# Pinning a pair's preparation to program order and moving the weights' low parts ahead on VectorE, in a two-layer RWKV-7 and attention encoder

## The chip, the cores and the metric

The kernel runs on one core of one Trainium2 chip. The metric is the device time in microseconds of one execution; lower is better. TensorE is PE in the profile (its weight loads PEld), VectorE is DVE, ScalarE is ACT, GpSimd is POOL and SyncE, which issues the DMAs, is SP.

## The reference

Two layers over 256 tokens of width 2048, all in float32. Each layer normalizes, multiplies by one input matrix, runs two groups of heads side by side and multiplies by one output matrix:

```python
for l in range(DEPTH):
    h = rms_norm(x, norm_g[l])
    proj = jnp.einsum('btd,dc->btc', h, w_in[l])
    rw_in, g_rw, q, k_at, v_at, g_at = jnp.split(proj, col_splits, axis=-1)
    rw_in = bidir_token_shift(rw_in, shift_mu[l])
    r, k, v, xw, xa = jnp.split(rw_in, rw_splits, axis=-1)
    y_rw = rwkv7_branch(r, k, v, xw, xa, ...)      # 16 heads of 64, a scan in each direction
    ...
    y_at = window_attention(qh, kh, vh, sink[l])   # 16 heads, 4 of keys and values
    mix = jnp.concatenate([y_rw * silu(g_rw), y_at * silu(g_at)], axis=-1)
    x = x + jnp.einsum('btc,cd->btd', mix, w_out[l])
return rms_norm(x, final_g)
```

One step of the scan, per head, with a 64x64 state S:

```python
s_kk = einsum('bhvk,bhk->bhv', S, kk_t)
S = S * w_t - s_kk * (a_t * kk_t) + v_t * k_t
y_t = einsum('bhvk,bhk->bhv', S, r_t)
```

The decay w, the rate a and the normalized key kk are made from the projections by two low-rank products, tanh, exp and a sum over each head.

## The kernel before, in words

**The gemm stream.** Both matrix products are one stream of steps (`Stream`, `gemm`). A tile is 128 output columns by 256 tokens, made in 16 steps over K = 2048. Each step is three matmuls (L273, L274, L275), because every operand is split into a high and a low part: high weights by high x, high weights by low x, low weights by high x. The third one needs `lo`. Weights come in halves of 8 steps. For each half, `wload` issues a DMA into `raw` (3 buffers), and `wsplit` makes `hi` on ACT (L215) and `lo` on DVE (L216), in two pieces of 512 columns, into 2 buffers each. A half is loaded and split (traced, that is) when 2 steps of the half before are left (`PREFETCH`). When a tile is done its eviction is traced: for k, v and r one DVE multiply (L400), an ACT scale (L401) and two DVE shifts (L402, L403); v also splits the low-rank weights of its pair (L442 on ACT, L443 on DVE); for the gate L411 to L413. The accumulators have 2 banks in PSUM.

**The windows.** The RWKV heads are done in 8 pairs. `window` cuts 64 gemm steps, four tiles, into 14 slots. In each slot it first advances the generators that are due, in this order: `scan_b` (the scan along 4 chunks, one step a slot), `scan_i` (what is inside a chunk; inverts triangular blocks by doubling, one level in two slots: L815, L817, L821, L823, then L824 and L825 on DVE), and last `scan_p`. Then it runs that slot's gemm steps. A pair passes `scan_p` in one window, `scan_i` in the next, `scan_b` behind it, so in the steady state three pairs are in work at once.

**The preparation, `scan_p`.** Its steps are in slots 4, 5, 6, 7, 8, 9, 10, 11 and 13 (`STAGE_P`):

- slot 4: the low-rank matmuls (L623 to L625), then on ACT L645, L648 twice, L650, L652
- slot 5: on DVE L655 and two running sums (L658)
- slot 6: head sums on PE (L629), ACT exponentials L664, L665, DVE reciprocal L667 and L668
- slot 7: DVE L675, L676, ACT L677 to L679
- slots 8, 9 and 10: DVE L681, L684; L686, L687 and ACT L688; L690 and ACT L694, L695
- slots 11 and 13: DVE L699, L700; head sums on PE and L705

Its results BK and MV are first read by `scan_i` at L720, in slot 0 of the next window.

**What sets the order.** The order of PE is the order in which the program is traced (`manual_schedule`). The order of each other engine is made ahead of time by a list scheduler: of the instructions that its own timing model holds ready, it issues the one with the lowest priority number, and that number is the instruction's place in the traced program. `tc.high_priority(offset=n)` moves a block's numbers n places ahead. `scan_b` has 95 (`PRIO_B`), the norm 100, all else none. So a piece whose inputs are ready early may be issued long before the place where it is traced. Once made, an engine's order is fixed in the program. The `lo` of L216 is traced in `wsplit` behind its `hi`:

```python
A.activation(hi[:, q], raw[:, q], AF.Copy)
V.tensor_tensor(lo[:, q], raw[:, q], hi[:, q].bitcast(F32), op=ALU.subtract)
```

At the end of a layer's windows come attention (`scores`, `flip`, `values`) and the output product, which is gemm stream alone.

Of the kernel before, what the change touches and what calls it, by code (L numbers as in the profile page):

```python
# [9 lines left out]
F32 = mybir.dt.float32  # L10
# [5 lines left out]
AF = mybir.ActivationFunctionType  # L16
ALU = mybir.AluOpType
# [4 lines left out]
T = 256  # L22
# [9 lines left out]
DECAY_C = -0.5 * float(np.exp(-0.5))  # L32
# [3 lines left out]
P_NG, P_MU0, P_MU1, P_KK, P_KA, P_RK, P_LG, P_LB, P_A0 = 0, 16, 42, 68, 76, 84, 92, 100, 108  # L36
P_N = 124
NSH = 26
# [12 lines left out]
    [0, 2, 5, 7, 8, 10, 12, 13],  # L51
]
PRIO_B = 95
PREFETCH = 2


# [72 lines left out]
def hybrid_trunk_kernel(ctx, tc, xT, wi, wv, wo, par, fing, dup, iup, sink, pos, cst, out):  # L129
    nc = tc.nc  # L130
    V, A, G, PE, SY = nc.vector, nc.scalar, nc.gpsimd, nc.tensor, nc.sync
# [73 lines left out]
    def wload(src):  # L205
        raw = wrp.tile([128, 1024], F32, tag="raw", name="raw")
        SY.dma_start(out=raw, in_=src)
        return raw

    def wsplit(raw):  # L210
        hi = wsp.tile([128, 1024], F32R, tag="hi", name="hi")
        lo = wsp.tile([128, 1024], F32R, tag="lo", name="lo")
        for i in range(2):
            q = slice(i * 512, (i + 1) * 512)
            A.activation(hi[:, q], raw[:, q], AF.Copy)  # L215
            V.tensor_tensor(lo[:, q], raw[:, q], hi[:, q].bitcast(F32), op=ALU.subtract)  # L216
        return hi, lo

    def halves(src, first=None):
        return [lambda: wsplit(first if first is not None else wload(src[0])), lambda: wsplit(wload(src[1]))]  # L220

    class Stream:


        def __init__(self):
            self.q = []
            self.ready = []
            self.timers = []
# [159 lines left out]
    def queue_inputs(l):  # L388
# [218 lines left out]
    def layer(l):  # L607
        L = layers[l]
        prm = lambda o, j: PR[:, l, o + j : o + j + 1]
        dpm = lambda o, j: DP[:, l, o + j : o + j + 1]  # L610
# [11 lines left out]
        def low_rank(o, w, x):  # L622
            PE.matmul(o, w[0], x[0], start=True, stop=False)  # L623
            PE.matmul(o, w[0], x[1], start=False, stop=False)
            PE.matmul(o, w[1], x[0], start=False, stop=True)  # L625

        def head_sums(o, x):
            for r in half:
                PE.matmul(o[r, 0:T], bones[r, r], x[r, 0:T], start=True, stop=True)  # L629


        def scan_p(p, t):
            K, VV, R, iu, du = t["k"], t["v"], t["r"], t["iu"], t["du"]
            dd = lambda x: x.rearrange("p (d x) -> p d x", d=2)
            two = lambda x: x.unsqueeze(1).to_broadcast([128, 2, T])
            c8 = lambda x: x.rearrange("p (n j) -> p n j", j=64)

            pza = wpair("pza")
            pz, pa = pza[:, 0], pza[:, 1]
            for d in range(2):  # L640
                low_rank(pz[:, d * T : (d + 1) * T], [a[0 : RANK + 1, d, :] for a in du], [a[0 : RANK + 1] for a in L.TW])
            LW = st("lw", [2 * T])
            for d in range(2):
                low_rank(pa[:, d * T : (d + 1) * T], [a[0:RANK, d, :] for a in iu], [a[0:RANK] for a in L.XA])
            A.activation(LW, pz, AF.Tanh, scale=0.5)  # L645
            TH = st("th", [2 * T])
            for d in range(2):
                A.activation(TH[:, d * T : (d + 1) * T], pa[:, d * T : (d + 1) * T], AF.Tanh, scale=0.5, bias=dpm(NSH + 16, d * 8 + p))  # L648
            sq = st("t1", [T], bufs=3)
            A.activation(sq, K, AF.Square, scale=prm(P_KK, p))  # L650
            KR = st("kkr", [T])
            A.activation(KR, K, AF.Identity, scale=prm(P_KK, p))  # L652
            yield

            V.tensor_scalar(LW, LW, 1.0, None, op0=ALU.add)  # L655
            msk = MSK.rearrange("p c j -> p (c j)")
            for x in (LW[:, 0:T], LW[:, T : 2 * T][:, ::-1]):
                V.tensor_tensor_scan(x, msk, x, 0.0, op0=ALU.mult, op1=ALU.add)  # L658
# [5 lines left out]
            A.activation(PP.rearrange("p d c j -> p (d c j)"), LW, AF.Exp, scale=DECAY_C)  # L664
            A.activation(IP.rearrange("p d c j -> p (d c j)"), LW, AF.Exp, scale=-DECAY_C)  # L665
            KD = st("kd", [T])
            V.reciprocal(KD, pk[:, 0:T])  # L667
            V.scalar_tensor_tensor(KD, KD, 1e24, KR, op0=ALU.min, op1=ALU.mult)  # L668
# [6 lines left out]
            V.scalar_tensor_tensor(MV[:, 0, :, 0, 1:64], PP[:, 0, :, 0:63], -1.0, kr4[:, :, 1:64], op0=ALU.mult, op1=ALU.mult)  # L675
            V.scalar_tensor_tensor(MV[:, 1, :, 0, 0:63], PP[:, 1, :, 1:64], -1.0, kr4[:, :, 0:63], op0=ALU.mult, op1=ALU.mult)  # L676
            A.activation(MV[:, 0, :, 0, 0:1], kr4[:, :, 0:1], AF.Copy, scale=-1.0)  # L677
            A.activation(MV[:, 1, :, 0, 63:64], kr4[:, :, 63:64], AF.Copy, scale=-1.0)
            A.activation(km, TH, AF.Identity, scale=dpm(NSH, p), bias=dpm(NSH + 8, p))  # L679
            yield  # L680
            V.scalar_tensor_tensor(dd(TH), dd(TH), 1.0, two(KD), op0=ALU.add, op1=ALU.mult)  # L681
            BK8 = BK.rearrange("p d c s j -> p (d c) s j")
            IP8 = IP.rearrange("p d c j -> p (d c) j")
            V.scalar_tensor_tensor(BK8[:, :, 1, :], c8(TH), 0.5, IP8, op0=ALU.mult, op1=ALU.mult)  # L684
            yield
            V.tensor_tensor(dd(km), dd(km), two(K), op=ALU.mult)  # L686
            V.tensor_tensor(BK8[:, :, 2, :], c8(km), IP8, op=ALU.mult)  # L687
            A.activation(BK8[64:128, :, 0, :], BK8[64:128, :, 2, :], AF.Copy)  # L688
            yield
            V.tensor_tensor(  # L690
                MV[:, :, :, 1, :], R.rearrange("p (c j) -> p c j", j=64).unsqueeze(1).to_broadcast([128, 2, NC, 64]), PP, op=ALU.mult
            )
            PC = st("pc", [2, NC], bufs=3)
            A.activation(PC[:, 0, :], PP[:, 0, :, 63], AF.Copy)  # L694
            A.activation(PC[:, 1, :], PP[:, 1, :, 0], AF.Copy)  # L695
            yield


            V.tensor_tensor(km[:, 0:T], km[:, 0:T], km[:, T : 2 * T], op=ALU.add)  # L699
            V.scalar_tensor_tensor(km[:, 0:T], km[:, 0:T], prm(P_RK, p), R, op0=ALU.mult, op1=ALU.mult)  # L700
            yield
            pb = wbank("pbn")
            head_sums(pb, km)
            bv = st("bv", [T], bufs=3)
            V.tensor_tensor(bv, pb[:, 0:T], VV, op=ALU.mult)  # L705
            t.update(BK=BK, MV=MV, PC=PC, bv=bv)
            yield

# [349 lines left out]
    for a, b in ((0, 2), (2, 4), (4, 8), (8, 12), (12, 16)):  # L1058
        x = X2[:, a:b, :]
# [83 lines left out]
```

## Time and profile before

| | |
|---|---|
| median of 3 runs | 1253.78 us (1252.38 to 1256.28) |
| the profiled execution's own time | 1253.19 us |
| its span, first to last instruction | 1251.3 us |
| PE busy | 1186.6 us (95%) |
| DVE busy | 928.8 us (74%) |
| ACT busy | 747.3 us (60%) |
| low parts (L216) | 560 of 685 ns |
| high parts (L215) | 560 of 624 ns |
| reciprocals of the preparation (L667) | 16 of 1755 ns |
| mean granted TensorE clock | 0.993 |

In the profile a row of the timeline reads: start, duration, engine, line, operation, out<-in, form, count, and in brackets how long the engine was idle before and what released it. A row of the waits reads: who waited, on whom, us in total, times, longest. Idle time of an engine that is not the bottleneck costs nothing by itself.

### The profile page before, as it was taken

Reading aid. Unit: us, or ns where it says so; the run is one execution under the profiler, and the core shown is the slowest. Engines: PE = TensorE matmul, PEld = TensorE weight load, DVE = VectorE, ACT = ScalarE, POOL = GpSimd, SP = SyncE. Lnnn points to the kernel's source line nnn. Section 1 sums busy time; section 2 is a strip of 40 time slices with the busy share of each in tenths; the row PEclk is TensorE's granted clock in tenths of the full one; section 3 lists DMA queues with packets and bytes.
Section 4 is the critical chain, followed back from the end, with each engine's and each line's share of the span. In section 5 each row is a group of like instructions: output and inputs, shape, how many; then the busy total and the mean of one; then the engine's idle time right before and its main releaser. Section 6 shows DMA issues by size and latency. Waiting matters only on the chain. (4 is left out here: it accounts for less than half of the span.)

```text
span 1251.3 us, 38155 instructions
## 1 busy us (share of the span) xinstructions
PE 1186.6 (95%) x16204; PEld 1094.6 (87%) x16204; DVE 928.8 (74%) x2067; ACT 747.3 (60%) x1838; POOL 19.0 (2%) x23
## 2 busy tenths in 40 slices
PE   6989999999999999999999999999999999999996
PEld 6978888888888889999998888888888888899996
DVE  7878878887886668856676878878887766786654
ACT  6556665666566566645555655665666565665553
POOL 0000000000000000000000000000000000000000
PEclk9999999999999999999999999999999999999998
DMA  7443233322323434466654433223322333335663
GB/s 246 158 141 124 96 103 109 103 83 102 120 86 97 135 110 141 140 216 230 202 186 141 135 124 116 89 92 110 103 92 92 118 107 124 134 132 173 209 192 119
DMA packets 60411, 166.72 MB, mean 133 GB/s; under 512 B 7728, under 2 KB 22736, under 8 KB 60240
## 3 DMA queue, kind: packets, MB, share of 16 engines
q1 hardware_dynamic: 60240, 164.27, 39.9%
q8 instruction: 127, 2.08, 0.7%
q14 instruction: 44, 0.36, 0.1%
HBM read 157.43 MB, written 4.19 MB: 129 GB/s over the span
## 5 line engine op out<-in xcount | busy, mean ns | idle before, releaser
L273 PE MATMUL pm<-XH,hi 128*128 128x256 f32 x1664 | 495.9, 298 | 13.9 <-ACT XH L178 6.4
L275 PE MATMUL pm<-XH,lo 128*128 128x256 f32 x1664 | 470.6, 283 | 20.0 <-DVE lo L216 19.9
L274 PE MATMUL pm<-XL,hi 128*128 128x256 f32 x1664 | 468.6, 282 | 0.1
L215 ACT ACTIVATE hi<-raw 128x512 fp32r<-128x512 f32 x560 | 326.7, 624 | 201.6 <-PE pm L274 163.1
L216 DVE TENSOR_TENSOR lo<-raw,hi 128x512 fp32r<-128x512 f32 x560 | 367.8, 685 | 104.1 <-ACT hi L215 95.7
L273 PEld LDWEIGHTS pm<-XH,hi 128*128 128x128 f32 x1664 | 314.5, 189 | 40.0 <-issue 13.0
L275 PEld LDWEIGHTS pm<-XH,lo 128*128 128x128 f32 x1664 | 315.1, 189 | 25.7 <-DVE lo L216 25.6
L274 PEld LDWEIGHTS pm<-XL,hi 128*128 128x128 f32 x1664 | 315.0, 189 | 0.8 <-DVE XL L179 0.8
L273 PE MATMUL pm<-MH,hi 128*128 128x256 f32 x512 | 144.8, 283 | 1.6 <-ACT hi L215 1.6
L275 PE MATMUL pm<-MH,lo 128*128 128x256 f32 x512 | 144.6, 282 | 0.4 <-DVE lo L216 0.4
L274 PE MATMUL pm<-ML,hi 128*128 128x256 f32 x512 | 144.5, 282 | 0.0
L273 PEld LDWEIGHTS pm<-MH,hi 128*128 128x128 f32 x512 | 97.4, 190 | 2.6 <-ACT hi L215 1.8
L275 PEld LDWEIGHTS pm<-MH,lo 128*128 128x128 f32 x512 | 97.3, 190 | 0.6 <-DVE lo L216 0.6
L274 PEld LDWEIGHTS pm<-ML,hi 128*128 128x128 f32 x512 | 97.3, 190 | 0.0
L888 ACT ACTIVATE suv<-pcc 64x128 f32<-64x128 f32 x128 | 34.4, 269 | 16.2 <-PE pq L815 10.9
L968 ACT ACTIVATE mv<-mv,mx 128x257 f32<-128x257 f32 x64 | 31.9, 503 | 16.3 <-DVE mx L965 16.2
L726 DVE TENSOR_TENSOR ge<-pg,C 128x1024 f32<-128x1024 f32 x32 | 39.0, 1218 | 3.0 <-PE pg L720 3.0
L735 ACT ACTIVATE AB<-ge 64x512 f16<-64x512 f32 x32 | 20.1, 629 | 30.9 <-DVE ge L726 30.5
L720 PE MATMUL pg<-mv,bk 64*128 64x128 f32 x512 | 37.2, 285 | 0.0
L824 DVE CAST_PREDICATED tv<-LV,pd 128x256 f16<-128x256 uint8 x80 | 34.1, 426 | 1.7 <-PE pd L823 1.2
L817 ACT ACTIVATE QF<-pq 128x256 f16<-128x256 f32 x80 | 30.9, 386 | 6.9 <-PE pq L815 5.9
L825 DVE CAST_PREDICATED tt<-LV,pd 128x256 f16<-128x256 uint8 x80 | 34.0, 424 | 0.0
(240 smaller groups left out, 1843.6 us busy)
## 6 DMA issues: line engine op xcount, KB each, us to landing
raw<-wi SPq DMA_DIRECT2D x207, 512.0 KB, 3.4
raw<-wo SPq DMA_DIRECT2D x64, 512.0 KB, 3.3
raw<-wv SPq DMA_DIRECT2D x8, 512.0 KB, 3.2
rrot<-u SPq DMA_DIRECT2D x80, 32.0 KB, 1.9
vg<-xT SPq DMA_DIRECT2D x16, 128.0 KB, 4.1
xd<-vg SPq DMA_DIRECT2D x16, 128.0 KB, 3.3
vg<-xd SPq DMA_DIRECT2D x16, 128.0 KB, 3.3
g<-dup SPq DMA_DIRECT2D x16, 97.0 KB
```

The source lines that it names most:

```text
L215: A.activation(hi[:, q], raw[:, q], AF.Copy)
L216: V.tensor_tensor(lo[:, q], raw[:, q], hi[:, q].bitcast(F32), op=ALU.subtract)
L273: PE.matmul(pm, wh, rh[:, kk, :], start=(kk == 0), stop=False)
L274: PE.matmul(pm, wh, rl[:, kk, :], start=False, stop=False)
L275: PE.matmul(pm, wl, rh[:, kk, :], start=False, stop=(kk == 15))
L720: PE.matmul(pg[:, h, c * 128 : (c + 1) * 128], BK[half[h], d, c, 1 - h : 3 - h, :].rearrange("p s j -> p (s j)"), MV[half[h], d, c].rearra ...
L726: V.tensor_tensor(GEd(d), pg.rearrange("p h (c x) -> p h c x", c=NC), gm[d].unsqueeze(1).unsqueeze(1).to_broadcast([128, 2, NC, 128]), op= ...
L817: A.activation(t_sub(QF), flat4(pq[:, :, 0:128]), AF.Copy)
L824: V.copy_predicated(t_sub(TC), t_mask, flat4(pd[:, :, 0:128]))
L825: V.copy_predicated(v_sub(TT), v_mask, flat4(pd[:, 0, 128:384].rearrange("p (d x) -> p d x", d=2)))
L888: A.activation(here(h), pc[half[h], 1], AF.Copy)
L968: A.activation(Sc[:, h, q, 0:257], Sc[:, h, q, 0:257], AF.Exp, scale=0.125, bias=mx[:, q : q + 1], accum_out=den[:, q : q + 1])
```

## The change

Two edits. The low parts of the weights get a priority 40 places ahead of where they are traced. And every ACT and DVE instruction of `scan_p` goes through a wrapper that ties it behind the last instruction traced before it on its engine (an edge of issue order; it waits for no result and adds no semaphore). The matmuls of `scan_p`, and all of `scan_i`, `scan_b`, the evictions and the high parts are left as they are.

```diff
 PRIO_B = 95
+PRIO_LO = 40
 PREFETCH = 2
...
             A.activation(hi[:, q], raw[:, q], AF.Copy)
-            V.tensor_tensor(lo[:, q], raw[:, q], hi[:, q].bitcast(F32), op=ALU.subtract)
+            with tc.high_priority(offset=PRIO_LO):
+                V.tensor_tensor(lo[:, q], raw[:, q], hi[:, q].bitcast(F32), op=ALU.subtract)
...
+    class InTurn:
+        def __init__(self, engine):
+            self.engine = engine
+        def __getattr__(self, name):
+            return lambda *a, **k: tc.keep_in_program_order(getattr(self.engine, name)(*a, **k))
+
+    PA, PV = InTurn(A), InTurn(V)
...
         def scan_p(p, t):
...
-            A.activation(LW, pz, AF.Tanh, scale=0.5)
+            PA.activation(LW, pz, AF.Tanh, scale=0.5)
...
-            V.tensor_scalar(LW, LW, 1.0, None, op0=ALU.add)
+            PV.tensor_scalar(LW, LW, 1.0, None, op0=ALU.add)
...
-            V.reciprocal(KD, pk[:, 0:T])
+            PV.reciprocal(KD, pk[:, 0:T])
...
```

The lines left out replace `A.` by `PA.` and `V.` by `PV.` in the same way, in all of `scan_p`.

More of the change, by code (lines that the diff above doesn't have):

```diff
@@ L644, in scan_p @@
                 low_rank(pa[:, d * T : (d + 1) * T], [a[0:RANK, d, :] for a in iu], [a[0:RANK] for a in L.XA])
-            A.activation(LW, pz, AF.Tanh, scale=0.5)
+            PA.activation(LW, pz, AF.Tanh, scale=0.5)
             TH = st("th", [2 * T])
             for d in range(2):
-                A.activation(TH[:, d * T : (d + 1) * T], pa[:, d * T : (d + 1) * T], AF.Tanh, scale=0.5, bias=dpm(NSH + 16, d * 8 + p))
+                PA.activation(TH[:, d * T : (d + 1) * T], pa[:, d * T : (d + 1) * T], AF.Tanh, scale=0.5, bias=dpm(NSH + 16, d * 8 + p))
             sq = st("t1", [T], bufs=3)
-            A.activation(sq, K, AF.Square, scale=prm(P_KK, p))
+            PA.activation(sq, K, AF.Square, scale=prm(P_KK, p))
             KR = st("kkr", [T])
-            A.activation(KR, K, AF.Identity, scale=prm(P_KK, p))
+            PA.activation(KR, K, AF.Identity, scale=prm(P_KK, p))
             yield
-            V.tensor_scalar(LW, LW, 1.0, None, op0=ALU.add)
+            PV.tensor_scalar(LW, LW, 1.0, None, op0=ALU.add)
             msk = MSK.rearrange("p c j -> p (c j)")
             for x in (LW[:, 0:T], LW[:, T : 2 * T][:, ::-1]):
-                V.tensor_tensor_scan(x, msk, x, 0.0, op0=ALU.mult, op1=ALU.add)
+                PV.tensor_tensor_scan(x, msk, x, 0.0, op0=ALU.mult, op1=ALU.add)
             yield
@@ L674, in scan_p @@
             kr4 = KR.rearrange("p (c j) -> p c j", j=64)
[L675 to L679, printed above, removed]
+            PV.scalar_tensor_tensor(MV[:, 0, :, 0, 1:64], PP[:, 0, :, 0:63], -1.0, kr4[:, :, 1:64], op0=ALU.mult, op1=ALU.mult)
+            PV.scalar_tensor_tensor(MV[:, 1, :, 0, 0:63], PP[:, 1, :, 1:64], -1.0, kr4[:, :, 0:63], op0=ALU.mult, op1=ALU.mult)
+            PA.activation(MV[:, 0, :, 0, 0:1], kr4[:, :, 0:1], AF.Copy, scale=-1.0)
+            PA.activation(MV[:, 1, :, 0, 63:64], kr4[:, :, 63:64], AF.Copy, scale=-1.0)
+            PA.activation(km, TH, AF.Identity, scale=dpm(NSH, p), bias=dpm(NSH + 8, p))
             yield
-            V.scalar_tensor_tensor(dd(TH), dd(TH), 1.0, two(KD), op0=ALU.add, op1=ALU.mult)
+            PV.scalar_tensor_tensor(dd(TH), dd(TH), 1.0, two(KD), op0=ALU.add, op1=ALU.mult)
             BK8 = BK.rearrange("p d c s j -> p (d c) s j")
             IP8 = IP.rearrange("p d c j -> p (d c) j")
-            V.scalar_tensor_tensor(BK8[:, :, 1, :], c8(TH), 0.5, IP8, op0=ALU.mult, op1=ALU.mult)
+            PV.scalar_tensor_tensor(BK8[:, :, 1, :], c8(TH), 0.5, IP8, op0=ALU.mult, op1=ALU.mult)
             yield
-            V.tensor_tensor(dd(km), dd(km), two(K), op=ALU.mult)
-            V.tensor_tensor(BK8[:, :, 2, :], c8(km), IP8, op=ALU.mult)
-            A.activation(BK8[64:128, :, 0, :], BK8[64:128, :, 2, :], AF.Copy)
+            PV.tensor_tensor(dd(km), dd(km), two(K), op=ALU.mult)
+            PV.tensor_tensor(BK8[:, :, 2, :], c8(km), IP8, op=ALU.mult)
+            PA.activation(BK8[64:128, :, 0, :], BK8[64:128, :, 2, :], AF.Copy)
             yield
-            V.tensor_tensor(
+            PV.tensor_tensor(
                 MV[:, :, :, 1, :], R.rearrange("p (c j) -> p c j", j=64).unsqueeze(1).to_broadcast([128, 2, NC, 64]), PP, op=ALU.mult
@@ L693, in scan_p @@
             PC = st("pc", [2, NC], bufs=3)
-            A.activation(PC[:, 0, :], PP[:, 0, :, 63], AF.Copy)
-            A.activation(PC[:, 1, :], PP[:, 1, :, 0], AF.Copy)
+            PA.activation(PC[:, 0, :], PP[:, 0, :, 63], AF.Copy)
+            PA.activation(PC[:, 1, :], PP[:, 1, :, 0], AF.Copy)
             yield
-            V.tensor_tensor(km[:, 0:T], km[:, 0:T], km[:, T : 2 * T], op=ALU.add)
-            V.scalar_tensor_tensor(km[:, 0:T], km[:, 0:T], prm(P_RK, p), R, op0=ALU.mult, op1=ALU.mult)
+            PV.tensor_tensor(km[:, 0:T], km[:, 0:T], km[:, T : 2 * T], op=ALU.add)
+            PV.scalar_tensor_tensor(km[:, 0:T], km[:, 0:T], prm(P_RK, p), R, op0=ALU.mult, op1=ALU.mult)
             yield
@@ L704, in scan_p @@
             bv = st("bv", [T], bufs=3)
-            V.tensor_tensor(bv, pb[:, 0:T], VV, op=ALU.mult)
+            PV.tensor_tensor(bv, pb[:, 0:T], VV, op=ALU.mult)
             t.update(BK=BK, MV=MV, PC=PC, bv=bv)
```

6 lines of the change are left out of this document (3 added, 3 removed).

## The prediction

> **What bounds the kernel now.** I read the page first (busy shares, the granted clock by slice), then the chain that ended last, then the waits of TensorE, then the same waits stretch by stretch, and last the timeline around one stall of each kind.
>
> ```profile
> span 1251.3 us, 38155 instructions
> PE 1186.6 (95%) x16204; PEld 1094.6 (87%) x16204; DVE 928.8 (74%) x2067; ACT 747.3 (60%) x1838; POOL 19.0 (2%) x23
> PEclk9999999999999999999999999999999999999998
> ```
>
> TensorE (PE) is busy 95% of the span at full clock, and its order is written by hand, which this change does not touch. So the change can only give back time in which PE waits, or add to it; 1251.3 - 1186.6 = 64.7 us is all the idle time there is. The chain that ended last says "issue" for its long middle, so it doesn't split those 65 us. The waits of PE do (who waited, on whom: us in total, times, longest):
>
> ```profile
> PE pm L275 <- DVE lo L216: 20.3, 27, 1.6
> PE pcc L893 <- ACT suv L888: 10.0, 11, 1.7
> PE pm L273 <- ACT hi L215: 4.7, 4, 1.7
> PE pm L273 <- DVE VA L523: 3.1, 2, 1.6
> ```
>
> The biggest is the low part of the weights, the very instruction that the change moves ahead. The same view for the first windows of layer 0 (55 to 80 us) and its steady ones (80 to 345):
>
> ```profile
> PE pm L275 <- DVE lo L216: 3.2, 3, 1.6
> PE pm L273 <- ACT hi L215: 0.8, 1, 0.8
> ```
>
> ```profile
> PE pm L275 <- DVE lo L216: 4.9, 6, 0.8
> PE pcc L893 <- ACT suv L888: 3.4, 4, 0.8
> PE pq L815 <- DVE tv L824: 0.7, 2, 0.4
> ```
>
> and for layer 1 (675 to 700, then 700 to 960):
>
> ```profile
> PE pm L275 <- DVE lo L216: 3.1, 5, 1.4
> PE pm L273 <- ACT hi L215: 0.7, 1, 0.7
> ```
>
> ```profile
> PE pm L275 <- DVE lo L216: 4.9, 6, 0.8
> PE pcc L893 <- ACT suv L888: 3.4, 4, 0.8
> PE pq L815 <- DVE tv L824: 0.7, 2, 0.4
> ```
>
> The reader should see how regular this is: in a steady window of about 44 us there is one 0.8 us stall on a low part and, from the third window on, one 0.8 us stall on L888, each time at the same place.
>
> **The stall on the low part.** VectorE (DVE) ahead of it, and the matmul that waited:
>
> ```profile
> 277.28 1.76 DVE L667 RECIPROCAL kd<-pk 128x256 f32<-128x256 f32 x1
> 278.95 0.63 DVE L216 TENSOR_TENSOR lo<-raw,hi 128x512 fp32r<-128x512 f32 x1
> ...
> 281.28 0.69 DVE L681 SCALAR_TENSOR_TENSOR th<-th,kd 128x512 f32<-128x512 f32 x1
> 281.89 0.48 DVE L403 SCALAR_TENSOR_TENSOR vg<-u,PR,vg 128x255 f32<-128x255 f32 x1
> 282.28 0.68 DVE L684 SCALAR_TENSOR_TENSOR bk<-th,ip 128x512 f32<-128x512 f32 x1
> 282.88 1.29 DVE L216 TENSOR_TENSOR lo<-raw,hi 128x512 fp32r<-128x512 f32 x2
> ```
>
> ```profile
> 283.62 0.39 PE L275 MATMUL pm<-XH,lo 128*128 128x256 f32 x1 [0.81 <-DVE lo L216]
> ```
>
> DVE is never idle here; the two splits of 282.88 stand last in a row of work. Three of the pieces ahead, L667, L681 and L684, are the preparation of a pair (`scan_p`).
>
> **The stall on L888.** ScalarE (ACT), the matmuls and DVE around it:
>
> ```profile
> 272.66 0.63 ACT L664 ACTIVATE pp<-lw 128x512 f32<-128x512 f32 x1 [1.53 <-DVE lw L658]
> 273.20 0.54 ACT L888 ACTIVATE suv<-pcc 64x128 f32<-64x128 f32 x2
> ...
> 276.37 0.39 ACT L817 ACTIVATE QF<-pq 128x256 f16<-128x256 f32 x1
> ```
>
> ```profile
> 273.79 0.45 PE L893 MATMUL pcc<-suv,bt 128*64 128x64 f32 x8 [0.84 <-ACT suv L888]
> ...
> 274.49 0.30 PE L815 MATMUL pq<-tv,AB 64*64 64x32 f16 x16
> 274.91 0.65 PE L629 MATMUL pk<-t,C 64*64 64x256 f32 x4
> ```
>
> ```profile
> 273.32 0.42 DVE L675 SCALAR_TENSOR_TENSOR mv<-pp,kkr 128x252 f32<-128x252 f32 x1 [0.70 <-ACT pp L664]
> ...
> 274.00 0.44 DVE L824 CAST_PREDICATED tv<-LV,pd 128x256 f16<-128x256 uint8 x1
> ...
> 275.33 0.69 DVE L686 TENSOR_TENSOR lw<-lw,kr 128x512 f32<-128x512 f32 x1
> ```
>
> L664 is preparation of slot 6, yet it stands in ACT's queue ahead of L888 of slot 5, and waits 1.53 us for DVE while L888 is stuck behind it. On DVE, L675 of slot 7 ran before L824 of slot 5.
>
> **The change part by part.** No instruction is added or removed: 2067 on DVE and 1838 on ACT stay, as do all matmuls and DMAs. Two orders change.
>
> *Preparation in program order.* Each ACT or DVE instruction of `scan_p` now comes behind the last instruction traced before it on its engine. For L664 that is L817 of the same slot, which needs L815, which PE reaches only after L893, which needs L888. So L664 can't stand ahead of that L888 any more: the 0.84 us stall must go, 4 + 4 times, 3.4 + 3.4 = 6.8 us. What comes in front of L888 instead is L650 and L652, pinned behind L648:
>
> ```profile
> L652 ACT ACTIVATE kkr<-kr,PR 128x256 f32<-128x256 f32 x16 | 8.1, 506 | 13.6 <-DVE kd L668 13.6
> L650 ACT ACTIVATE t<-kr,PR 128x256 f32<-128x256 f32 x16 | 8.0, 500 | 1.4 <-DVE kr L403 1.4
> ```
>
> L648 ends 1.53 us before L664 starts, at 271.13; 0.50 + 0.51 us of these and 0.54 of L888 end at 272.7, and L893 would start at 273.79 - 0.84 = 272.95. It fits with 0.27 us to spare; two high parts (L215) in between would cost up to 1 us. I take 0, between 0 and 8 x 1.0.
>
> L655 comes behind L825 of slot 5 and L675 behind L825 of slot 7. So L824 of a slot no longer waits for preparation of the same or a later slot: the stalls of L815 go, 0.7 + 0.7 = 1.4 us. And L675, L676, L690, L686, which ran between 273.3 and 276.0 ahead of the reciprocal, move to slots 7 to 10; L667 then starts soon after its matmuls (L629, at 274.91), about 2 us earlier than 277.28. In the last preparing window of each layer the reciprocal is what PE's third wait stands behind:
>
> ```profile
> 365.23 1.76 DVE L667 RECIPROCAL kd<-pk 128x256 f32<-128x256 f32 x1
> 366.90 0.39 DVE L523 TENSOR_SCALAR VA<-pva,rt 128x256 f32<-128x256 f32 x1
> ```
>
> With the reciprocal 1.4 to 2 us earlier the 1.55 us wait goes in both layers: 3.1 us, between 0 and 3.1.
>
> What a later preparation costs: its results are read by PE at the head sums of slots 6 and 13 and at L720 of the next window's slot 0. L684 and L687, the last that L720 reads, belong to slots 8 and 9, L690 to slot 10; three slots of 44 / 14 = 3.2 us cover them. Without that cover a preparing window would lose up to one slot, 3.2 us. I take 0.
>
> *Low parts 40 places ahead.* `lo` is traced inside slot 8's third gemm step here; behind L681 and L684 stand some two steps of 3 matmuls and a split, fewer than 40 places, so both splits now go ahead of L681 and L684 where they are ready together. That is 0.69 + 0.68 = 1.37 us of a wait of 0.81, and the earlier reciprocal adds to it. The steady stalls go: 4.9 + 4.9 = 9.8 us. In the first windows of each layer (3.2 + 3.1 = 6.3 us) there is no `scan_i` yet to hold preparation back, and slots are shorter by its matmuls; a reciprocal of 1.76 us that has begun isn't interrupted. I take half, 3.1, between 0 and 6.3. The ACT waits there (0.8 + 0.7) I leave as they are: L650 and L652 stay ahead of the high part; between 1.5 us better and 1.0 worse.
>
> What is queued behind an earlier `lo`: evictions (L400 to L403, with a whole tile, 44 / 4 = 11 us, until their bank is wanted), L824 and L825 (wanted one slot later) and, through the raw buffer, SP's next weight load, which only comes earlier.
>
> *What takes the place.* DVE has more to do per unit of time once PE runs on (columns: PE, PEld, DVE, ACT, POOL busy in one window):
>
> ```profile
> 253.60:297.80 44.20, 42.42 (x759) 38.24 (x754) 35.41 (x74) 28.26 (x74) 1.01 (x1) 1.00 0.31 100
> ```
>
> 35.41 of 44.2 us is 80%; of 42.55 us it would be 83%. It still isn't the bound, but new waits are likely. Bounds: none, or one of 0.82 us in each of 16 preparing windows, 13 us. I charge 0.25 us a window, 4 us, nearer to none, since the preparation is spread out where it was bunched.
>
> **Sum.** 6.8 + 1.4 + 3.1 + 9.8 + 3.1 - 4 = 20.2 us off the profiled execution's 1253.19 us (span 1251.3 and 1.9 around it): 1233.0. The median of the runs shown is 0.6 higher, so 1233.6. If all goes (the 24.2 us with the other 3.1 of the first windows and 1.5 on ACT, no new wait) 28.9 us: 1225; with 13 us of new waits 11.2 us: 1242.6.
>
> **The rivals.**
>
> *Only ACT's half works.* Preparation moved into slots 7 to 10 meets the evictions of the tile that ends with slot 6, and the low part is as late as before. For it: L681 and L684 were already in the slots where they are traced, and `lo` can only overtake what is ready with it. Then 6.8 + 1.4 + 3.1 - 4 = 7.3 us: 1246.5.
>
> *A blocked head, slower.* DVE takes its instructions in order, and a `lo` at its head that waits for its high part holds everything behind it:
>
> ```profile
> DVE lo L216 <- ACT hi L215: 95.7, 104, 2.6
> ```
>
> That is 0.92 us each, today with little urgent behind. If more low parts stand ahead of L824, the hand-off from L823 to the next slot's L815 grows. There are 5 a window and 16 windows: 80. From 24.2 / 80 = 0.30 us a hand-off on the change loses; at 0.4 us it is 32 - 24.2 = 8 us slower, 1262. Against it: L815 waited on L824 for 1.4 us in all steady windows, so the cover (most of a slot's 3.2 us) is mostly unused. [...]
>
> *Nothing that can be measured.* PE finds another wait for each that goes; or a pin on only the last traced instruction holds little, because that one itself ran early. Against it: L817 and L825 can't run early, PE feeds them. About 1252.
>
> **How the numbers follow.** Most stalls go, 1223 to 1243: 0.65. Only ACT's half, 1243 to 1250: 0.17. No measurable change (0.3%, 3.8 us, is about what a measurement of this kernel can tell from none): 0.07. Slower: 0.11. Hence faster 0.82, same 0.07, slower 0.11. 1223 to 1249 leaves out the last two cases and a little of the first two; the likeliest one's own range is 1223 to 1243.
>
> **What would show it.** Right: no wait of PE on L888 in the windows with a preparation (3.4 and 3.4 us gone), L664 behind L817, L675 behind L825, L667 within 1 us of its head sums, PE's waits on `lo` below 8 us, none on L523. The window's period goes from 44.3 to about 42.7 us. Wrong: `lo` waits of 0.8 us at a new place in each window, L815 waiting on L824 or L893 on L888 tens of times, or DVE's idle time on L215 well above 95.7 us.

## The result and the profile after

The changed kernel takes 1237.39 us (median of 4 runs, 1236.29 to 1238.08), the kernel before, run beside it, 1254.72. The ratio is 0.9863 [0.9844, 0.9881]: 1.4% faster. The forecast was 1233.6 us in 1223 to 1249.

The head of the page of the changed kernel:

```profile
span 1235.3 us, 38135 instructions
PE 1182.8 (96%) x16204; PEld 1095.8 (89%) x16204; DVE 928.9 (75%) x2067; ACT 745.1 (60%) x1838; POOL 19.1 (2%) x23
```

Every engine runs as many instructions as before; the span is 16.0 us shorter. A note on lines: the page of the changed kernel puts every ACT and DVE instruction of `scan_p` down to L231, the line of the wrapper, so they are told apart by their tiles. The other lines moved by 2 to 14: `lo` is L218 (L216 before), the gemm L286 to L288 (L273 to L275), the head sums L642 (L629), `tv` L838 (L824), its matmul L829 (L815), `pf` L845 (L831), and `suv` L902 with L907 (L888 with L893).

PE's waits of the changed kernel, whole span (who waited, on whom: us in total, times, longest):

```profile
PE pk L642 <- ACT t L231: 5.9, 2, 3.5
...
PE pm L288 <- DVE lo L218: 5.6, 9, 1.5
PE pbn L642 <- DVE lw L231: 5.6, 2, 2.8
PE pq L829 <- DVE tv L838: 4.0, 4, 1.3
...
PE pf L845 <- DVE tv L838: 2.6, 2, 2.1
PE pcc L884 <- DVE suv L909: 2.5, 3, 1.2
PE pf L845 <- DVE tt L839: 2.1, 2, 1.4
...
PE pcc L907 <- ACT suv L902: 1.6, 2, 0.8
...
PE pm L286 <- DVE VA L536: 0.5, 2, 0.2
```

Against the rows of before: `lo` 20.3 to 5.6, `suv` 10.0 to 1.6, `VA` 3.1 to 0.5, so 25.7 us of waits are gone. Between the third and the eighth of the starts listed below, in either layer, no row of PE's waits is left. The first, third and fourth rows are waits that the kernel before did not have or had smaller; they eat a good part of it. For those that had a row before, the kernel before:

```profile
PE pf L831 <- DVE tv L824: 2.0, 2, 1.1
PE pq L815 <- DVE tv L824: 1.9, 6, 0.4
...
PE pf L831 <- DVE tt L825: 0.7, 2, 0.4
PE pcc L870 <- DVE suv L895: 0.5, 1, 0.5
```

**Where it came from.** PE runs the same 16204 matmuls in the same order in both kernels, so the start of one and the same matmul can be compared, and the difference of two starts holds every delay between them. I take the first low-rank matmul (`pza<-TW,duh`) of each of the eight windows that prepare a pair. Timeline of PE, before and then after, the sixth window of layer 0:

```profile
266.68 0.38 PE L623 MATMUL pza<-TW,duh 97*128 97x256 f32 x1
```

```profile
262.35 0.38 PE L636 MATMUL pza<-TW,duh 97*128 97x256 f32 x1
```

All sixteen starts (us); in the steady windows the period went from 44.3 to 42.0 us:

| | layer 0 | layer 1 |
|---|---|---|
| before | 59.7 95.3 134.7 178.2 222.4 266.7 311.0 355.3 | 671.4 707.0 746.4 789.9 834.2 878.4 922.7 967.0 |
| after | 59.6 97.9 136.3 178.3 220.3 262.4 304.4 346.4 | 661.3 701.9 740.4 782.4 824.4 866.4 908.4 950.5 |
| difference | -0.1 +2.6 +1.6 +0.1 -2.1 -4.3 -6.6 -8.9 | -10.1 -5.1 -6.0 -7.5 -9.8 -12.0 -14.3 -16.5 |

So the two layers' steady windows (third to eighth start) gave 10.5 + 10.5 = 21.0 us; the first two windows of the layers took back 1.7 + 4.1 = 5.8 us (the first windows alone got longer by 2.7 and 5.0, the second ones shorter by 1.0 and 0.9); the stretch from the last preparation of layer 0 to the first of layer 1 gave 1.2, and the rest is -0.4. That is the 16.0.

### The profile page after: what moved, and what is told of

Read it like the earlier page. It is cut to its first block, busy times and chain, and to the rows that moved or that the text cites. A ratio compares the mean times of both kernels' runs of the same rounds, so it can differ in the third digit from the quotient of the medians.

```text
span 1235.3 us, 38135 instructions
## 1 busy us (share of the span) xinstructions
PE 1182.8 (96%) x16204; PEld 1095.8 (89%) x16204; DVE 928.9 (75%) x2067; ACT 745.1 (60%) x1838; POOL 19.1 (2%) x23
## 5 line engine op out<-in xcount | busy, mean ns | idle before, releaser
L286 PE MATMUL pm<-XH,hi 128*128 128x256 f32 x1664 | 498.7, 300 | 9.4 <-ACT XH L179 5.8
L288 PE MATMUL pm<-XH,lo 128*128 128x256 f32 x1664 | 471.5, 283 | 5.2 <-DVE lo L218 5.2
L216 ACT ACTIVATE hi<-raw 128x512 fp32r<-128x512 f32 x560 | 327.9, 624 | 212.4 <-PE pm L287 157.3
L218 DVE TENSOR_TENSOR lo<-raw,hi 128x512 fp32r<-128x512 f32 x560 | 369.4, 687 | 110.9 <-ACT hi L216 103.4
L286 PEld LDWEIGHTS pm<-XH,hi 128*128 128x128 f32 x1664 | 317.0, 191 | 35.7 <-issue 13.2
L288 PEld LDWEIGHTS pm<-XH,lo 128*128 128x128 f32 x1664 | 317.6, 191 | 7.3 <-DVE lo L218 6.8
L286 PE MATMUL pm<-MH,hi 128*128 128x256 f32 x512 | 143.9, 281 | 1.1 <-ACT hi L216 1.1
L288 PE MATMUL pm<-MH,lo 128*128 128x256 f32 x512 | 143.7, 281 | 0.4 <-DVE lo L218 0.4
L286 PEld LDWEIGHTS pm<-MH,hi 128*128 128x128 f32 x512 | 96.4, 188 | 2.0 <-ACT hi L216 1.3
L288 PEld LDWEIGHTS pm<-MH,lo 128*128 128x128 f32 x512 | 96.4, 188 | 0.6 <-DVE lo L218 0.6
L902 ACT ACTIVATE suv<-pcc 64x128 f32<-64x128 f32 x128 | 34.6, 270 | 18.4 <-PE pq L829 13.4
L831 ACT ACTIVATE QF<-pq 128x256 f16<-128x256 f32 x80 | 30.9, 386 | 20.3 <-PE pq L829 19.6
L838 DVE CAST_PREDICATED tv<-LV,pd 128x256 f16<-128x256 uint8 x80 | 34.5, 431 | 7.4 <-PE pd L837 6.6
L886 ACT ACTIVATE rh<-pcc 128x128 f32<-128x128 f32 x64 | 17.5, 273 | 33.7 <-PE pcc L884 33.3
```

The costliest lines, as they stand in the source:

```text
L286: PE.matmul(pm, wh, rh[:, kk, :], start=(kk == 0), stop=False)
L288: PE.matmul(pm, wl, rh[:, kk, :], start=False, stop=(kk == 15))
L831: A.activation(t_sub(QF), flat4(pq[:, :, 0:128]), AF.Copy)
L838: V.copy_predicated(t_sub(TC), t_mask, flat4(pd[:, :, 0:128]))
L902: A.activation(here(h), pc[half[h], 1], AF.Copy)
```

## The experiments

Two theories at the start. **A**: the pins do all the good; the low parts' priority adds nothing on top and makes waits elsewhere. **B**: both edits are needed, the pins for L888 and the priority for `lo`. Later ones ask why the first windows lost, and which engine's pins are needed.

### e1_lo_alone and e2_pins_alone: one edit each

```diff
  # e1: the kernel before, with only
+            with tc.high_priority(offset=PRIO_LO):
                 V.tensor_tensor(lo[:, q], raw[:, q], ...)
  # e2: the change, without that line
```

> The low parts 40 places ahead, the preparation left as before. Main theory (each edit gives its own part): the twelve steady waits on lo go (9.8 us) with some of the 6.3 us of the first windows, the eight waits of L893 on L888 (6.8 us) and the two behind L523 (3.1 us) stay, and lo in front of L824 costs about 4.6 us in the windows of the keys and queries: 9 us faster, about 1245. Rival A (the pins do everything, by taking the bunch of preparation away): the steady waits on lo stay, 1250 to 1256. Rival B (the low parts do everything): 1237, like the change.

> The preparation in program order, the low parts left at their place. Main theory: waits on L888 and behind L523 go (about 9.5 us), the steady waits on lo come back in part (0 to 9.8 us), the head sums of each layer's first preparing window wait as in the change (about 11.5 us and the half clock after them), and the 4.6 us of L845 and L829 behind lo in the windows of the keys and queries are saved: 1237 to 1246. Rival A (the pins do everything): no steady wait on lo, 1232 to 1235. Rival B (the low parts do everything): 1254 or slower, since the first windows' losses stay.

Measured: e1 1250.72 us, 0.9976 [0.996, 0.9991]; e2 1233.23 us, 0.9838 [0.982, 0.9857]. The pins alone give at least what the change gives (intervals overlap); the priority alone gives 0.24%. The time of e1 is the one that its rival A named, but not for rival A's reason, which was that the steady waits on `lo` would stay. Waits of e1's PE in the steady windows of layer 0 (80 to 345 us):

```profile
PE pcc L895 <- ACT suv L890: 3.4, 4, 0.8
PE pq L817 <- DVE tv L826: 2.9, 7, 0.4
PE pbn L631 <- DVE lw L702: 1.7, 1, 1.7
```

No `lo` row is left, so the priority does cure the 4.9 us there. But `tv` went from 0.7 to 2.9 and `lw` is new. DVE of e1 shows how:

```profile
279.27 1.28 DVE L218 TENSOR_TENSOR lo<-raw,hi 128x512 fp32r<-128x512 f32 x2
...
282.89 0.69 DVE L218 TENSOR_TENSOR lo<-raw,hi 128x512 fp32r<-128x512 f32 x1
283.62 0.42 DVE L826 CAST_PREDICATED tv<-LV,pd 128x256 f16<-128x256 uint8 x1
```

Two low parts now run ahead of the preparation (279.27), as meant, and the next one runs ahead of `tv` (L826), which PE wants at once (it waits 0.43 us for it, at 284.09). The same stretch in e2:

```profile
PE pm L287 <- DVE lo L217: 0.9, 2, 0.6
PE pbn L641 <- DVE lw L230: 0.9, 1, 0.9
```

Pins alone take the `lo` waits from 4.9 to 0.9 as well: the preparation that stood ahead of the low part is now spread over its own slots. Theory A holds for the steady windows. The two edits cure the same stall; they don't add up. On the new wait of `pbn` they do: over the whole span it is 3.2 us in e1, 3.0 in e2 and 5.6 with both. And without the priority the waits behind `tv` and `suv` on DVE are small: in e2 `tv` ahead of `pq` is 0.4 in all (4.0 in the change), `pf` 3.5 (4.7) and the matmul L884 of the change 0.3 (2.5).

### e3_first_pair_free and e4_and_lo_in_windows: where the first windows lose

```diff
  # e3, in scan_p
+            PA, PV = (InTurn(A), InTurn(V)) if p > 0 else (A, V)
  # e4: e3, and the priority only while pairs are prepared
-            with tc.high_priority(offset=PRIO_LO):
+            with tc.high_priority(offset=PRIO_LO if ahead[0] else 0):
```

> As the change, but the first pair of each layer is prepared without pins. Main theory (the pins cost the first preparing window of each layer its waits of L642, 5.9 us on ACT and 5.6 us on DVE, and three stretches of half clock behind them, 1.7 us each): those 16.6 us go, and part of the 7.8 us that this window waited for lo and hi before comes back: 1224 to 1231. Rival (the time was only moved: DVE is too full there, and what doesn't wait at L642 waits at lo): 1236 to 1239.

> As the run with the first pair free, and the low parts are ahead only as long as pairs are prepared (not from the window behind the last preparation to the layer's end of attention). Main theory: L845, L829 and L884 no longer wait behind low parts in the windows of the keys and queries; 4.6 us and the half clock at 1015 us (1.7 us) go: 4 to 6 us faster than the run with the first pair free alone. Rival (those waits come from the earlier arrival of PE, not from the order): the same as that run within 1.5 us.

Measured: e3 1231.43 us, 0.9824 [0.9803, 0.9846]; e4 1226.31 us, 0.9777 [0.976, 0.9795]. Whole-span waits of e3:

```profile
PE pm L288 <- DVE lo L218: 7.4, 11, 1.4
...
PE pq L830 <- DVE tv L839: 4.4, 4, 1.3
...
PE pbn L642 <- DVE lw L715: 3.2, 2, 1.7
```

The wait of `pk` (5.9 in the change) is gone: the pins of the first pair made it. `pbn` is 3.2 instead of 5.6, which is what the priority makes of it without any pin (e1). The time is just outside the forecast. By the starts of the same matmuls the first window of layer 1 is 36.1 us long in e3 (40.6 in the change, 35.6 before), but that of layer 0 is still 37.9 (38.2 and 35.6): two stretches of half clock stand in it (71.2 and 84.8; last section). With the priority gone as well (e8, below) the two are 35.4 and 35.2. e4 takes another 5.1 us off by leaving the low parts at their old place everywhere outside the preparing windows. Where it comes from: between 345 and 445 us, where the attention's Q and K gemms meet the last pairs, PE's waits fall from 7.1 to 4.2 us (`tv` and `tt` ahead of `pf` 3.0 to 2.4, `tv` ahead of `pq` 1.2 to 0.3, `suv` 2.1 to 1.0), and near the end of layer 1's scans a wait of 1.3 on `tv` (at 1009.9) falls to 0.4, and the stretch of half clock at it is gone (1.7 us, last section). In those stages the priority only costs.

### e6_act_pins and e7_dve_pins: which engine's pins

```diff
-    PA, PV = InTurn(A), InTurn(V)
+    PA, PV = InTurn(A), V         # e6
+    PA, PV = A, InTurn(V)         # e7
```

> As the change, but only the preparation's ACT instructions are pinned, its DVE instructions are free. Main theory (PE's wait on L888 is a matter of ACT's order; the first head sums wait for a pinned L650, the last for a pinned L700): waits on L888 gone, L642 on ACT 5.9 us as in the change, L642 on DVE (5.6 us) gone or small; L675, L676 and L690 need L664, so DVE's bunch is broken up too and most steady waits on lo stay away: 1230 to 1236. Rival (the bunch on DVE must be pinned itself): steady waits on lo come back, up to 9.8 us, 1240 to 1246.

> As the change, but only the preparation's DVE instructions are pinned, its ACT instructions are free. Main theory: L642 on ACT (5.9 us and two stretches of half clock, 3.4 us) gone, L642 on DVE stays; L658 comes behind L825, so L664 is ready later than L888 in the scheduler's eyes and L888 keeps its place: 1226 to 1231. Rival (only a pin on ACT keeps L664 behind L888): eight waits of 0.84 us come back, 1233 to 1238.

Measured: e6 1231.57 us, 0.9808 [0.9785, 0.9831]; e7 1236.28 us, 0.9846 [0.9819, 0.9872]. Neither brings the stall on `suv` back in the steady windows, as expected; e7's rival, that only a pin on ACT keeps L664 behind L888, falls. The time of e7 misses its forecast all the same (1226 to 1231) and lies where the rival put it: `pk` is gone, but the mean granted clock is 0.989, as in the change (0.990; last section), and `lo` and `hi` wait 11.8 us where they waited 8.6. The chain is coupled: L664 (`pp`, ACT) waits for L658 (DVE), and L675 (DVE) waits for `pp`; hold either and the other can't run early. The waits of the first pair differ. e6, then e7, whole span:

```profile
PE pk L642 <- ACT t L231: 5.7, 2, 3.1
...
PE pbn L642 <- DVE lw L714: 2.4, 2, 1.5
```

```profile
PE pbn L642 <- DVE lw L231: 5.5, 2, 2.8
```

So `pk` belongs to the pins on ACT. Of `pbn`, the pins on DVE make a part: 2.4 us are left without them, which e1 has too, from the priority.

### e8_pins_later_pairs_only: e3 without the priority

```diff
+            PA, PV = (InTurn(A), InTurn(V)) if p > 0 else (A, V)
-            with tc.high_priority(offset=PRIO_LO):
```

> The first pair of each layer free, all others pinned, and no priority for the low parts at all. Theory after the first runs (the steady windows are mended by the pins; the low parts ahead only move waits to L824): steady windows as in the change, no L829-type wait behind lo in the windows of the keys and queries, the lo waits of each layer's first window as in the kernel before (6.3 us): 1224 to 1229. Rival (the low parts ahead are worth their 9.8 us once the pins spread the preparation): slower than the run with low parts ahead in the windows (1226.3) by 4 us or more.

Measured: 1226.11 us, 0.9762 [0.9742, 0.9783], the same as e4 and 0.4% below e3. Its waits:

```profile
PE pm L287 <- DVE lo L217: 13.0, 18, 1.6
...
PE pq L829 <- DVE tv L838: 0.7, 2, 0.4
```

13.0 us on `lo`, 7.4 in e3, and it is still faster: what the priority cures on `lo` it gives back elsewhere: on `tv` (4.4 in e3, 0.7 here), on `pbn` (3.2 in e3, no row here), and in half clock (three windows of 3.4 us in e3, two here; last section).

### e9_splits_pinned_too, e10_bonus_free, e11_later_pairs_splits: the two new waits

The timelines of the changed kernel at the first pair of layer 0, ACT and then PE:

```profile
65.56 0.42 ACT L455 ACTIVATE duh<-g 97x256 fp32r<-97x256 f32 x1 [4.96 <-DMA g<-dup]
...
66.19 0.57 ACT L231 ACTIVATE lw<-pza 128x512 f32<-128x512 f32 x1
66.67 0.82 ACT L231 ACTIVATE th<-pza,DP 128x256 f32<-128x256 f32 x2
67.38 0.50 ACT L231 ACTIVATE t<-kr,PR 128x256 f32<-128x256 f32 x1
```

```profile
67.94 0.65 PE L642 MATMUL pk<-t,C 64*64 64x256 f32 x4 [3.50 <-ACT t L231]
...
84.46 0.65 PE L642 MATMUL pbn<-lw,C 64*64 64x256 f32 x4 [2.78 <-DVE lw L231]
```

A split of the low-rank weights (L455, of a later pair, not pinned) has floated ahead on ACT and waits 4.96 us for its DMA. `t`, pinned, comes behind it and behind the two lines of its own pair, and PE's head sums 3.50 us late. The split waited for this DMA in the kernel before as well (4.33 us, at 65.00), at no cost to `pk`, because there the `t` of this pair had long been made:

```profile
39.00 0.49 ACT L650 ACTIVATE t<-kr,PR 128x256 f32<-128x256 f32 x1
```

The inputs of `t` are ready long before its place in the program; the pin moved it from 39.00 to 67.38, behind a wait that it had been far ahead of. For `pbn`, DVE:

```profile
81.25 1.29 DVE L218 TENSOR_TENSOR lo<-raw,hi 128x512 fp32r<-128x512 f32 x2
82.46 0.48 DVE L415 SCALAR_TENSOR_TENSOR kr<-u,PR,kr 128x255 f32<-128x255 f32 x1
82.97 0.48 DVE L416 SCALAR_TENSOR_TENSOR kr<-u,PR,kr 128x255 f32<-128x255 f32 x1
83.37 0.42 DVE L231 TENSOR_TENSOR lw<-lw 128x256 f32<-128x256 f32 x1
83.83 0.48 DVE L231 SCALAR_TENSOR_TENSOR lw<-lw,PR,kr 128x256 f32<-128x256 f32 x1
```

The two additions that feed it (L713, L714; 83.37 and 83.83) stand behind two low parts and two evictions. Three kernels take these apart:

```diff
  # e9: the change, and the splits of the low-rank weights pinned
-        def split(hl, x, rows):
+        def split(hl, x, rows, A=A, V=V):
...
-                    split(t[n], raw, rows)
+                    split(t[n], raw, rows, PA, PV)
  # e10: e9's split, no priority for lo, and the two additions free
-            PV.tensor_tensor(km[:, 0:T], ...)
+            V.tensor_tensor(km[:, 0:T], ...)
  # e11: e8 with e9's split
```

> As the change, and the split of the next pair's low-rank weights (L455 on ACT, L456 on DVE in the changed kernel) is pinned to program order as well. Theory: in each layer's first preparing window L455 stood in ACT's queue ahead of the pinned L645, L648 and L650 and waited 4 to 5 us for its DMA; pinned behind the eviction of v it comes after them, L650 is early, and the waits of the first head sums (3.5 and 2.4 us) go, with one or two stretches of half clock (1.7 us each): 1227 to 1232. Rival (L650 is late by the pins themselves, not by the DMA): those waits stay, 1236 to 1239.

> Pins without the priority of the low parts (1233.2 us by itself), the splits of the low-rank weights pinned too, and L699 and L700 free again. Theory (the first head sums waited for a DMA through ACT's order, the last ones for L700 pinned behind the evictions of r in a slot too short for it): waits on the first head sums 6.0 us and on the last 3.0 us go, with up to three stretches of half clock (1.7 us each): 1221 to 1226. Rival (DVE is simply full in each layer's first preparing window): the last head sums or lo wait instead, 1228 to 1233.

> The first pair free, no priority for the low parts (1226.1 us by itself), and the splits pinned to program order. If what the first pair still waits for is the high part behind the split that waits for its DMA (2.9 us) and the low part behind preparation (6 us), the first goes and the second stays: 1222 to 1225. If the split's place is of no account without pins on the first pair: 1226.

Measured: e9 1231.18 us, 0.9803 [0.9779, 0.9828]; e10 1226.25 us, 0.9766 [0.9753, 0.978]; e11 1226.05 us, 0.9767 [0.9753, 0.978]. e9 and e10:

```profile
PE pbn L642 <- DVE lw L231: 7.8, 2, 4.1
...
PE pk L642 <- ACT t L231: 1.4, 1, 1.4
```

```profile
PE pm L287 <- DVE lo L217: 11.1, 16, 3.2
```

e9: with the splits in turn `pk` falls from 5.9 to 1.4; the cause is shown. `pbn` grows to 7.8; why was not taken apart. e10: with the additions free and no priority `pbn` has no row left (the pins without the priority, e2, had 3.0), and `lo` waits 11.1, one of 3.2 us at 670.7 behind seven pieces of preparation. Its time is a quarter of a microsecond above the forecast. In the first window of a layer, then, the piece that comes last on DVE is the one PE waits for. It is not that DVE has more work there than the window holds: it is busy 27.4 of 38.2 us in the change's first window, and in e12 below 26.9 of 32.5 us in layer 1's. e11 is e8 again (1226.11): with the first pair free the splits don't matter.

### e12_act_pins_splits and e13_act_pins_splits_lo: pins on ACT only

```diff
-            with tc.high_priority(offset=PRIO_LO):            # e12: gone
+            with tc.high_priority(offset=PRIO_LO if ahead[0] else 0):   # e13
-    PA, PV = InTurn(A), InTurn(V)
+    PA, PV = InTurn(A), V
-                    split(t[n], raw, rows)
+                    split(t[n], raw, rows, PA, PV)
```

> Only ACT's half of the preparation pinned, the splits' ACT half pinned, no priority for the low parts. Theory (DVE needs no pin, since L675, L676 and L690 follow L664; the low parts ahead only cost): the run with ACT pins (1231.6) less the first head sums (5.7 us and 3.4 us of half clock) and less some 4 us behind low parts in the windows of the keys and queries: 1217 to 1223. Rival (with free DVE instructions it was the priority that kept the low parts on time): the steady waits on lo come back, 9.8 us, 1226 to 1232.

> As the run before in this list, but with the low parts 40 places ahead as long as pairs are prepared. Theory: the same within 2 us, with the 1 us waits of the second preparing window on L838 in place of waits on lo: 1217 to 1224. Rival (the priority keeps the low parts on time where DVE is free): 5 to 10 us faster than the run without it.

Measured: e12 1217.44 us, 0.970 [0.9686, 0.9713]; e13 1216.5 us, 0.970 [0.9682, 0.9718]. Both are 3.0% faster than the kernel before and by the medians 1.6 to 1.7% below the change. They can't be told apart. The engines of e12, whose span is 1215.5 us, and its waits:

```profile
PE 1176.4 (97%) x16204; PEld 1089.8 (90%) x16204; DVE 926.5 (76%) x2067; ACT 747.9 (62%) x1840; POOL 18.9 (2%) x23
```

```profile
PE pm L287 <- DVE lo L217: 7.8, 11, 1.3
...
PE pk L641 <- ACT t L230: 1.4, 1, 1.4
```

There is no row for `pbn`; e13, with the priority, has one of 4.0. e10 differs from e12 in the pins on DVE alone (all but its two additions have them), so these cost 8.8 us by the medians (1226.25 and 1217.44). By the starts of the same matmuls e12's steady windows are as long as the change's (41.9 and 42.0 us); the 19.8 us between their spans come from elsewhere: 2.3 before the first preparation (not explained), 3.3 in the first window of layer 0 (34.9 us long, 38.2 in the change), 4.9 between the last preparation of layer 0 and the first of layer 1 (of which 3.0 are rows: the waits between 345 and 445 us are 3.8 in e12 and 6.8 in the change), and 8.1 in the first window of layer 1 (32.5 against 40.6). ACT in order carries the steady windows, and DVE free to take what is ready carries the first ones. With ACT alone pinned the priority, kept to the windows, is worth nothing that can be told (e13).

## Why the prediction was right, and where it was not

*L888, 6.8 us: right.* No steady window waits on `suv` (10.0 to 1.6 in all). ACT of the changed kernel:

```profile
269.59 0.38 ACT L831 ACTIVATE QF<-pq 128x256 f16<-128x256 f32 x1 [0.36 <-PE pq L829]
269.87 0.62 ACT L231 ACTIVATE pp<-lw 128x512 f32<-128x512 f32 x1
```

`pp` (L664 before) now stands behind the copy of its slot (L831, L817 before), as worked out. e6 and e7 add that it need not be ACT's own pin.

*L523 behind the reciprocal, 3.1 us: right, 2.6 came.* 3.1 to 0.5; in the eighth window, the one that counts, the reciprocal starts at 355.07 where it was 365.23, and the window itself started 8.9 us earlier, so 1.3 us of it are the change's, and the wait fell by as much, from 1.55 to 0.25. The 2 us were read off the sixth window (277.28 to 270.95, less 4.3); there 1.3 of the 2.0 come from the head sums, which no longer stand behind the stall on L888.

*Steady low parts, 9.8 us: the waits went, but not by the 40 places alone.* The prediction gave this to the 40 places. They do it by themselves (e1 has no such row in layer 0's steady windows), but so do the pins (e2, 0.9 us left there): the earlier reciprocal, which it named as an addition, and the preparation's later place are enough. So the 9.8 us are no part that the second edit adds.

*L824, 1.4 us: the stalls went, and a new one took their place.* The two stalls of 0.3 to 0.4 us in each layer's second window (101.17 and 106.71 before) are gone, as worked out. But the same window has a new wait of 0.97 us later on (117.99 and 722 us), with two evictions and two low parts ahead of `tv`; e2, without the priority, does not have it. In all this wait went from 1.9 to 4.0. DVE's idle time on high parts shows the same:

```profile
DVE lo L218 <- ACT hi L216: 103.4, 120, 2.6
```

95.7 us in 104 waits before, 103.4 in 120 now. This fits the blocked head that the slower rival named, at a small price: 2.1 us on `tv` of `pq`, and, with a longest of 2.1 where it was 1.1, 2.0 on `pf` (2.7 to 4.7) and 2.0 on L884 (0.5 to 2.5). That it is the low parts' place is shown by e2 (0.4, 3.5 and 0.3); that they blocked while waiting for their high part, rather than by their own time, is not shown. What stood at the head of a queue did hold what was behind it: in the kernel before, DVE was idle for 1.73 us up to 267.17 with a `lo` waiting for its high part, and behind it the eviction L400, whose tile PE had finished at 265.43, came at 267.78; in the change L455 with its 4.96 us stood ahead of `t`, for which PE waited 3.50 us. The loss that the rival worked out from it did not come: 1237.39, not 1262.

*The first windows, 3.1 us better: the step that failed.* They got 7.7 us worse (2.7 and 5.0), a miss of 10.8. The waits on `lo` and `hi` there fell from 7.8 to 1.5, but two things came that the sum did not have: the late head sums, 5.9 us on `pk` and 5.6 on `pbn`, and three stretches of half clock of about 1.7 us each, two of them behind head sums (69.5 and 687.3) and one behind a wait of 1.46 us on a low part (673.6). The term "What a later preparation costs ... I take 0" was wrong, twice over. It names the head sums of slots 6 and 13 as readers, but works out the cover of three slots for L720 alone, and off a steady window of 44 us; the first windows are 35.6 us long, 2.5 us a slot. And it asked only what a pinned instruction stands behind in program order, not what an instruction that is not pinned may put in front: L455 with its DMA. L650 was checked for what it delays (L888), not for what waits for it. The text's own bound (one slot, 3.2 us, a window) is near what came (2.4 to 3.5 us a wait, two waits in the first window of each layer); it was then not charged.

*New waits, 4 us: none where they were looked for.* They were charged to the preparing windows because DVE would be fuller. The steady ones have none, the second ones one of 0.97 us each; the large ones are the head sums of the first windows, accounted above, and the rest come behind the last preparation (`pf`, L884 and `tv`).

*The stalls were priced at their rows, and are worth more.* The prediction's 0.81 us wait was taken at its printed length. The matmul ahead of it, kernel before:

```profile
282.53 0.28 PE L274 MATMUL pm<-XL,hi 128*128 128x256 f32 x1
```

The next began at 283.62, 1.09 us later; with no stall such matmuls follow each other by 0.117 us (68.74, 68.86, 68.97 in the changed kernel). So 0.97 us were lost, 0.16 more than the row, whose idle time begins at the modelled end, 0.28 us after the start. In the sixth window, where the rows of the two stalls are 0.81 and 0.84, the time from its first matmul to that of the next fell by 2.25 us: 0.98 of it at the low part, 0.91 at L893, and the rest between the matmuls right behind L893. So the period came to 42.0 us, not the forecast 42.7.

Put by place, the sum's 20.2 became 16.0 like this (us gained, both layers):

| | in the sum | measured |
|---|---|---|
| first windows | 3.1 | -7.7 |
| second windows | 3.0 (`lo` 1.6, L824 1.4) | 1.9 |
| third to eighth start | 15.0 (`lo` 8.2, L888 6.8) | 21.0 |
| from the eighth start on, and the start | 3.1 (L523) | 0.8 |
| new waits | -4 | in the rows above |

So the total came near the forecast partly by luck: 6 us more in the steady windows than their rows say, and no charge needed there, against 10.8 less in the first ones.

*The rivals.* "Only ACT's half works" (1246.5) fell with the `lo` waits; yet something of its mechanism, that the preparation meets the evictions, is seen at `pbn` in the first window (the two evictions ahead of the additions, above). "Nothing that can be measured" fell: L817 and L825 hold what is pinned behind them.

## What to carry to other kernels

Two edits that cure the same stall are worth one of them: before both are made, ask what each does alone, and on which other queue heads it sits (here the priority added nothing to the pins and cost 5 us outside the preparing windows). When part of a work is tied to program order, look for what waits for a DMA on the same engine and can get in front, and ask of each tied piece how early it ran before and who waits for it. Here the engine that PE's last head sums wait for in the first windows, DVE, was better left free to choose: pins on ACT alone with its splits gave 3.0% where pins on both with the priority gave 1.4%. Price a move also by the window with the shortest slots, not by the steady one alone.

## What the hardware showed that was not expected

**Half clock after short gaps.** Behind some stalls PE ran at half rate for 3.4 us or twice that. Windows of the changed kernel (columns: PE, PEld, DVE, ACT, POOL busy, granted clock, DMA share, GB/s), in order the stretch behind the wait of 3.50 us, one around the 2.78 us wait at 84.46, and one at the end of layer 1:

```profile
69.50:72.90 3.40, 3.40 (x18) 3.40 (x18) 3.31 (x6) 3.40 (x9) 0.00 (x0) 0.51 0.02 8
81.00:86.00 5.00, 2.22 (x18) 1.66 (x17) 3.60 (x8) 1.14 (x3) 0.00 (x0) 1.00 0.66 212
...
1014.90:1018.30 3.40, 3.40 (x42) 3.18 (x43) 1.39 (x2) 1.63 (x4) 0.00 (x0) 0.51 0.35 131
```

The matmuls of one form, which start 0.117 us apart at 69.1, start 0.21 apart in the first stretch: by this spacing 1.5 us of its 3.4 were lost, by the granted clock of 0.51 1.7, which I take for each such stretch. What stood ahead of the last one:

```profile
1012.28 0.45 PE L884 MATMUL pcc<-suv,ge 128*64 128x64 f32 x8 [1.16 <-DVE suv L909]
...
1014.04 0.30 PE L829 MATMUL pq<-tv,AB 64*64 64x32 f16 x16 [1.30 <-DVE tv L838]
```

Two gaps of 1.16 and 1.30 us, with 0.46 us of work between them, were followed by half clock; a single one of 2.78 was not (clock 1.00 in 81 to 86), and one of 2.77 us just ahead of 687.3 was. Beyond the start and the end of the run the kernel before had one such stretch (558.2), the change four (69.5, 673.6, 687.3, 1014.9), e12 none, which is most of why PE's busy time is 1176.4 us there and 1182.8 in the change. In e9 two of them lasted twice as long (6.8 us, at 80.0 and 680.8). So in the change the waits of 3.50 and 2.77 us, and one of 1.46 (at 673.07), were each followed by 1.7 us lost beside themselves, and the wait of 2.78 us was not.

The traces narrow down what went with it. In those of the kernel before, the change, e2, e3, e9 and e13, every stretch of half clock begins on one grid of 3.413 us (in the change 69.45, 673.61, 687.26 and 1014.94 are 16, 193, 197 and 293 steps behind 14.84; in e9 680.76 and 1011.85 are 176 and 273 steps behind 80.01), and the phase of the grid against the kernel differs from trace to trace (counted from the start of the span 1.88 us before, 1.18 in the change, 0.21 in e2, 2.90 in e3). For the kernel before and the change I add up PE's idle rows over 0.05 us in each window of this grid that ran at full clock, leaving out the first 20 us and the last 15. All 4 windows with 1.75 us or more were followed by half clock (1.96 in the kernel before; 1.90, 2.06 and 2.78 in the change), 1 of the 6 with 1.45 to 1.75 (1.46, ahead of 673.61), and none of the 691 with less. In these two traces half clock thus went with the idle time in one window of the grid, 1.46 us or more, and not with the length of a single gap: the 2.78 us ahead of 84.46 lie across a boundary (83.11), 1.4 us in one window and 1.35 in the next; the 2.77 us ahead of 687.0 lie in one window whole. Since the phase differs, which of the gaps above cost half clock is in part luck of the execution that was profiled.

**Open besides.** Why `lo` still waits 7.8 us in e12 was not taken apart, and e13, which moves 4.6 us of it elsewhere at no gain in time, does not tell whether it can be had.
